# Experts' stage: queries' products and picks stepped inside the experts' loop, the row scale moved into the gates' exponent, norm sums taken from transposed tiles

## The chip, the cores and the metric

The kernel runs on one NeuronCore of a Trainium2 chip. The core has engines with instruction queues of their own: PE (TensorE, matrix products, whose weight loads the profile shows as PEld), DVE (VectorE), ACT (ScalarE), POOL (GpSimd) and SP (SyncE), and 16 DMA engines that move data between HBM and SBUF. Each engine takes its instructions in order and waits on semaphores. The metric is the device time of one execution, in microseconds (us).

## The reference, cut to what matters

Two transformer blocks over 256 tokens of 2048 values, all in float32. The change lies between them: in the expert layer (PEER) of the first block and in the two norms that follow it.

```python
def peer(xn, wq, subkeys, u, v):             # xn = rmsnorm(h, ffn_norm), 256 tokens
    q = (xt @ wq).reshape(T, 8, 2, 128)      # 8 heads, two halves of 128
    s1, s2 = q[:, :, 0] @ subkeys[0].T, q[:, :, 1] @ subkeys[1].T
    v1, i1 = top_k(s1, 16); v2, i2 = top_k(s2, 16)
    cand = (v1[..., :, None] + v2[..., None, :]).reshape(T, 8, 256)
    sc, ci = top_k(cand, 16)                 # 16 experts per head and token
    idx = i1[ci // 16] * 128 + i2[ci % 16]
    gate = softmax(sc)
    h = gelu(einsum('cd,chkd->chk', xc, u[idx]))
    return einsum('chk,chkd->cd', gate * h, v[idx])
h = h + peer(...)
x = rmsnorm(h, final_norm)                   # end of the first block
h2 = rms_norm(x, norm1_w)                    # start of the second
proj = h2 @ w_in                             # z, dt, conv input, q, k, v
```

## The kernel before

The 256 tokens lie as two tiles of 128 partitions (tt = 0 and 1). The weights stream from HBM through `Stream` (L36): chunks of 128x1024 floats (512 KB, `raw`, ring of 4, loaded by SP), each split into a rounded part `hi` on ACT (L64) and a rest `lo` on DVE (L70).

The stage that the change rebuilds is `peer`. It has three kinds of work:

- **Queries** (`queries`): 16 tiles `qT[0..15]` of 128x256, each from two chunks of `wq`. A chunk is 8 pairs of products on PE, L241 (512 columns) and L243 (256 columns). A finished tile is added up by ACT L253 and DVE L257, and multiplied on DVE by the row scale `rb` (L258).
- **Picks** (`picks`, `topk`): for each token tile and head, 16 in all, two small products (L968), then on DVE the best 16 of 128 twice, the best 16 of the 256 sums, and the indices `ix`; ACT takes the exponent of the scores (L1007).
- **Experts** (`experts`): 256 steps (tt, head, k), numbered e0 to e255 here. In each step POOL starts an indirect DMA (L866) that fetches, for each of the 128 tokens, one row of 4096 floats (u and v side by side, 2.1 MB a step) into one of NBUF = 5 buffers `uv`. DVE multiplies the u half with the gained tokens `hg` and sums (L926), ACT takes the gelu (L928), DVE makes the diagonal matrix `dg` (L907), PE adds `dg` times the v half into four PSUM banks (L909, four products, eight matmuls in the trace). The buffer is then free for the fetch four steps ahead. Head hh of tile tt needs the pick of that head before its first fetch.

`mix(queries(), experts(), MIXQ)` writes these out in code order: one step of `experts` for each chunk of the queries until the queries end. `experts` has three such steps for each expert, and more where a pick is missing. The code order isn't the engines' order: the framework puts each engine's instructions in an order of its own when it builds the program, and starts an instruction earlier than the code has it where its inputs and buffers are there. PSUM and SBUF buffers of a tag are handed out in code order.

After e127 `residual(0)` adds the four banks to `h` (L915) and frees them for tile 1; `turn(0, j)` then transposes `h` in 128x128 pieces (L879) and splits them for the second block (ACT L228, DVE L229), and `stats(0, j)` forms the sums of h squared and of (h times `fn`) squared for the two norms, with `fn` loaded from HBM in eight pieces (L893, L895, L212). The same follows for tile 1 after e255, beside the first products of the second block (`self.first`, L274 to L276).

At the start of `peer`, POOL forms `hg` = h times `fg` for both tiles (L825, eight multiplications of 128x512), and `spread` makes `rb` on PE and DVE (L164, L166).

## Time and profile before

| what | value |
|---|---|
| time, median of 3 runs | 2891.52 us (2889.49 to 2894.91) |
| time of the profiled execution | 2895.72 us |
| its span, first to last instruction | 2893.9 us |
| PE, DVE, ACT, POOL busy | 88%, 67%, 32%, 12% of the span |
| mean granted TensorE clock | 0.981 of full speed |
| DMA, mean over the span | 282 GB/s |
| indirect fetches (queue q0) | 536.89 MB, 44.1% of 16 DMA engines over the span |

The span lies 1.8 us under the profiled execution's own time, and that execution lies 4.2 us over the median of the three runs. Busy shares are means over stages with different limits, so the stage in question is read from windows of the trace: its first fetch starts 403 us into the span, its last expert's products end at 1755 us.

### The profile page before, as it was taken

The numbers are of one execution on the slowest core, as the hardware profiler recorded it, in microseconds if no ns is written. First come the engines' busy times: TensorE is split into PE (matmuls) and PEld (weight loads), VectorE is DVE, ScalarE is ACT, GpSimd is POOL, SyncE is SP. The second block draws the span as 40 slices with busy tenths as digits, with TensorE's granted clock in tenths as the row PEclk, the third lists the DMA queues.
The fourth block names the chain that finished last, engine by engine and source line by source line (L and its number), as shares of the span: only waits on it lengthen the run. The fifth ranks groups of instructions, "written<-read, shape, count | busy, mean of one in ns | idle before, by whom it ended". The sixth has DMA issues, their size and how long they took to land.

```text
span 2893.9 us, 29409 instructions
## 1 busy us (share of the span) xinstructions
PE 2554.5 (88%) x10286; PEld 1712.4 (59%) x10286; DVE 1947.3 (67%) x3558; ACT 927.0 (32%) x1665; POOL 349.8 (12%) x314
## 2 busy tenths in 40 slices
PE   9999999768777776877777778999999999999999
PEld 8877776323222222322222227888888888888887
DVE  6778677997555555555555555885668888887444
ACT  6556543221000002000000004555454444444333
POOL 0211031222121112211212110000000000000000
PEclk9999999989999998999999999999999999999999
DMA  8332478989999999999999995545455555555664
GB/s 318 117 102 89 148 277 347 384 320 380 427 428 429 428 428 374 428 428 428 429 428 427 428 428 181 195 132 181 156 182 183 188 187 184 188 184 188 197 195 154
DMA packets 119380, 817.34 MB, mean 282 GB/s; under 512 B 14656, under 2 KB 17600, under 8 KB 85696
## 3 DMA queue, kind: packets, MB, share of 16 engines
q0 software_dynamic: 36864, 536.89, 44.1%
q1 hardware_dynamic: 76032, 271.58, 28.5%
q10 hardware_dynamic: 6336, 6.99, 0.8%
q8 instruction: 81, 1.33, 0.2%
q14 instruction: 67, 0.55, 0.1%
HBM read 813.32 MB, written 2.10 MB: 282 GB/s over the span
## 4 chain that ended last, share of the span: by engine, by line
PE 46%; DMA 30%; issue 9%; DVE 8%; POOL 1%; ACT 1%; POOLq 0%; ACTq 0%; DVEq 0%
DMA uv<-in_uv_dram,ix 28%; PE acc L241 14%; PE acc L243 7%; PE acc L274 7%; PE acc L276 7%; PE acc L275 7%; DVE uv L926 2%; PE acc L909 2%; POOL uv L866 1%; DMA raw<-in_wq_dram 1%; DVE lo L70 1%; DMA fnc<-in_fn_dram 1%; DVE dg L907 0%; DVE tmp L959 0%; ACT hi L64 0%
## 5 line engine op out<-in xcount | busy, mean ns | idle before, releaser
L909 PE MATMUL acc<-uv,dg 128*128 128x512 f32 x2048 | 967.8, 618 | 298.0 <-DVE dg L907 298.0
L909 PEld LDWEIGHTS acc<-uv,dg 128*128 128x128 f32 x2048 | 379.4, 194 | 874.0 <-DVE dg L907 483.6
L926 DVE CUSTOM_DVE_ANT_0 uv<-uv,hg 128x2048 f32<-128x2048 f32 x256 | 586.4, 2291 | 372.9 <-DMA uv<-in_uv_dram,ix 372.8
L70 DVE TENSOR_TENSOR lo<-raw,hi 128x1024 fp32r<-128x1024 f32 (+3 forms) x494 | 597.2, 1210 | 315.5 <-ACT hi L64 314.1
L64 ACT ACTIVATE hi<-raw 128x1024 fp32r<-128x1024 f32 (+3 forms) x506 | 527.8, 1044 | 697.8 <-PE acc L276 270.1
L241 PE MATMUL acc<-xs,hi 128*128 128x512 f32 x1936 | 696.4, 402 | 0.0
L243 PE MATMUL acc<-xs,lo 128*128 128x256 f32 x1936 | 548.6, 283 | 0.0
L928 ACT ACTIVATE g<-d,rs 128x1 f32<-128x1 f32 x256 | 75.3, 294 | 1099.6 <-DVE d L926 1099.5
L241 PEld LDWEIGHTS acc<-xs,hi 128*128 128x128 f32 x1936 | 368.0, 190 | 90.5 <-issue 0.9
L866 POOL DMA_INDIRECT uv<-in_uv_dram,ix x256 | 271.3, 1060 | 1081.0 <-PE acc L909 509.1
L243 PEld LDWEIGHTS acc<-xs,lo 128*128 128x128 f32 x1936 | 367.7, 190 | 1.6 <-issue 0.8
L907 DVE TENSOR_SCALAR dg<-ident,g,gt 128x128 f32<-128x128 f32 x256 | 106.4, 416 | 97.3 <-ACT g L928 91.0
L274 PE MATMUL acc<-hi,xs 128*128 128x512 f32 (+3 forms) x384 | 147.1, 389 | 2.0 <-ACT hi L64 2.0
L275 PE MATMUL acc<-lo,xs 128*128 128x512 f32 (+3 forms) x384 | 144.3, 377 | 4.4 <-DVE lo L70 3.3
L276 PE MATMUL acc<-hi,xs 128*128 128x512 f32 (+3 forms) x384 | 143.0, 377 | 0.0
L276 PE MATMUL acc<-hi,act 128*128 128x512 f32 x352 | 138.7, 394 | 0.0
L274 PE MATMUL acc<-hi,act 128*128 128x512 f32 x352 | 138.7, 394 | 0.0
L275 PE MATMUL acc<-lo,act 128*128 128x512 f32 x352 | 138.7, 394 | 0.0
L241 PE MATMUL m<-xs,hi 128*128 128x512 f32 x256 | 96.5, 416 | 2.4 <-ACT hi L64 2.4
L1339 DVE SCALAR_TENSOR_TENSOR fu<-fup,fw,fu 128x256 f32<-128x256 f32 x176 | 84.8, 482 | 3.1
L275 PEld LDWEIGHTS acc<-lo,xs 128*128 128x128 f32 x384 | 74.0, 193 | 16.0 <-DVE lo L70 5.9
L274 PEld LDWEIGHTS acc<-hi,xs 128*128 128x128 f32 x384 | 73.7, 193 | 13.4 <-ACT hi L64 2.8
(319 smaller groups left out, 2332.0 us busy)
## 6 DMA issues: line engine op xcount, KB each, us to landing
raw<-in_w_up_dram SPq DMA_DIRECT2D x176, 512.0 KB, 3.3
raw<-in_w_dn_dram SPq DMA_DIRECT2D x88, 512.0 KB, 3.4
raw<-in_w_in_dram SPq DMA_DIRECT2D x66, 512.0 KB, 3.5
raw<-in_w_out_dram SPq DMA_DIRECT2D x64, 512.0 KB, 3.4
raw<-in_w_b_dram SPq DMA_DIRECT2D x48, 512.0 KB, 3.3
raw<-in_wq_dram SPq DMA_DIRECT2D x32, 512.0 KB, 4.5
raw<-in_w_z_dram SPq DMA_DIRECT2D x16, 352.0 KB, 3.5
btab<-in_btab_dram SPq DMA_DIRECT2D x4, 1024.0 KB, 7.9
```

The lines of the kernel that those rows point to most:

```text
L64: self.nc.scalar.activation(h[:, :n], r[:, :n], AF.Copy)
L70: e.tensor_tensor(lo[:, :n], r[:, :n], h[:, :n].bitcast(F32), op=ALU.subtract)
L241: nc.tensor.matmul(acc, h[:, s], x.rearrange("p a t -> p (a t)"), start=(kk == 0), stop=False, skip_group_check=True)
L243: nc.tensor.matmul(acc[:, T:], lo[:, s], x[:, 0], start=False, stop=(kk == nk - 1), skip_group_check=True)
L274: nc.tensor.matmul(a, x[:, 0, t], h[:, s], start=(kk == 0), stop=False, skip_group_check=True)
L275: nc.tensor.matmul(a, x[:, 0, t], lo[:, s], start=False, stop=False, skip_group_check=True)
L276: nc.tensor.matmul(a, x[:, 1, t], h[:, s], start=False, stop=(kk == nk - 1), skip_group_check=True)
L866: nc.gpsimd.indirect_dma_start(out=t, out_offset=None, in_=I["uv"], in_offset=bass.IndirectOffsetOnAxis(ap=idx[tt][hh][:, k:k + 1], axis=0))
L907: nc.vector.tensor_scalar(dg, self.ident, g, gate[tt][hh][:, k:k + 1], op0=ALU.mult, op1=ALU.mult)
L909: nc.tensor.matmul(out[tt][c], dg, t[:, D + c * 512:D + c * 512 + 512], start=(hh, k) == (0, 0), stop=(hh, k) == (7, 15), skip_group_check ...
L926: nc.vector.tensor_tensor_reduce(t[:, :D], t[:, :D], hg[:, tt], 1.0, 0.0, op0=ALU.mult, op1=ALU.add, accum_out=d)
L1339: nc.vector.scalar_tensor_tensor(u[a], up[:, j:j + T], w[:, j:j + 1], u[a], op0=ALU.mult, op1=ALU.add)
```

## The change

- **Order of the stage.** `mix` and `experts` are gone. `peer` writes the first two query tiles, then the pick for head 0 and four fetches, three more chunks of queries, and then the loop over the 256 experts. In it an even step writes one chunk of queries, an odd step one sixth of a pick and one step of the work after a tile. A fetch that lacks its pick writes pick steps, and query chunks where those wait.
- **Row scale.** The query tiles are no longer multiplied by `rb`: L258 (16 multiplications of 128x256 on DVE) and the first `spread` are gone. The order of the scores within a row stays, and the gates' exponent takes the row scale as its factor (`scale=r`, and `sm` = -r times the best score).
- **hg.** POOL forms `hg` for tile 0 only; for tile 1 it is `late_gains`, on DVE, written after e72.
- **Norm sums.** `stats` is gone. `turn` squares the transposed pieces on ACT with the gain as factor (16 pieces of 128x128 a token tile), and PE sums them over partitions with products of one column (`sums`); the sixteen loads of `fn` and the products and squares on them are gone. The sum of h squared stays.
- **Change of tile.** `residual(0)` is written in step 129, before the products of e128, instead of at the end of step 128.

```diff
--- before.py
+++ after.py
@@ -28,7 +28,6 @@
...
 MIX1 = 4.2
-MIXQ = 1.0
 MIX3 = 2.0
...
@@ -817,12 +816,19 @@
...
         hg = tk.tile([128, 2, D], F32, name="hg")
+        fgs = {}
+        def gained(tt, j, e):
+            e.tensor_tensor(hg[:, tt, 512 * j:512 * j + 512], h[:, tt, 512 * j:512 * j + 512], fgs.pop((tt, j)),
+                            op=ALU.mult)
+        def gains(tt, j):
+            fgs[tt, j] = fg = pw.tile([128, 512], F32, tag="fg", name="fg")
+            nc.scalar.dma_start(out=fg, in_=I["fg"][:, 512 * j:512 * j + 512])
         for j in range(4):
-            s = slice(512 * j, 512 * j + 512)
-            fg = pw.tile([128, 512], F32, tag="fg", name="fg")
-            nc.scalar.dma_start(out=fg, in_=I["fg"][:, s])
-            for tt in range(2):
-                nc.gpsimd.tensor_tensor(hg[:, tt, s], h[:, tt, s], fg, op=ALU.mult)
+            gains(0, j)
+            gained(0, j, nc.gpsimd)
         skT = tk.tile([128, 2, 128], F32, name="skT")
...
@@ -831,11 +837,7 @@
...
         def ev(i):
-            def f(a):
-                if i == 0:
-                    nm.spread()
-                self.add_halves(qT[i], a, pw, nm.rb)
-            return f
+            return lambda a: self.add_halves(qT[i], a, pw)
...
@@ -849,26 +851,33 @@
...
                     yield from self.until(f"pq{hh}")
-                    yield from self.topk(qT, skT, iota, tt, hh, idx[tt][hh], gate[tt][hh], tk)
+                    yield from self.topk(qT, skT, iota, rs, tt, hh, idx[tt][hh], gate[tt][hh], tk)
                     self.marks.add(f"pk{tt}{hh}")
...
         rows = {}
-        side = self.beside(picks())
+        main = queries()
+        side = picks()
...
             while f"pk{tt}{hh}" not in self.marks:
-                yield next(side)
+                if next(side) is WAIT:
+                    step(main)
             rows[i] = t = uvp.tile([128, 2 * D], F32, tag="uv", name="uv")
...
         n2 = self.nm = Norm(self, None, self.gains[:, 4], self.npool)
-        self.ss2 = self.npool.tile([128, 2, 8], F32, name="ss2")
+        self.ss2 = self.npool.tile([128, 2], F32, name="ss2")
+        fnT = tk.tile([128, 16], F32, name="fnT")
+        nc.vector.tensor_copy(fnT, self.gains[:, 4])
         nc.vector.tensor_tensor(self.gains[:, 4], self.gains[:, 4], self.gains[:, 2], op=ALU.mult)
+        one = tk.tile([128, 1], F32, name="one")
+        nc.vector.memset(one, 1.0)
+        sums = {}
...
@@ -884,16 +893,19 @@
...
-        def stats(tt, j):
+            sq = pw.tile([128, 512], F32, tag="fg", name="sq")
+            for k in range(4):
+                nc.scalar.activation(sq[:, k * 128:k * 128 + 128], p[:, k * 128:k * 128 + 128], AF.Square,
+                                     scale=fnT[:, 4 * j + k:4 * j + k + 1])
+            if j == 0:
+                sums[tt] = self.ps()
+            for k in range(4):
+                nc.tensor.matmul(sums[tt][:, :1], sq[:, k * 128:k * 128 + 128], one, start=(j, k) == (0, 0),
+                                 stop=(j, k) == (3, 3), skip_group_check=True)
+            yield
             self.sumsq(h[:, tt, 512 * j:512 * j + 512], n2.ssp[:, tt, j:j + 1])
-            for q in (2 * j, 2 * j + 1):
-                fn = pw.tile([128, T], F32, tag="fg", name="fnc")
-                cs = slice(T * q, T * q + T)
-                nc.scalar.dma_start(out=fn, in_=I["fn"][:, cs])
-                sq = pw.tile([128, T], F32, tag="a0", name="sq")
-                nc.vector.tensor_tensor(sq, h[:, tt, cs], fn, op=ALU.mult)
-                self.sumsq(sq, self.ss2[:, tt, q:q + 1])
+            if j == 3:
+                nc.vector.tensor_copy(self.ss2[:, tt:tt + 1], sums[tt][:, :1])
             yield
...
@@ -914,42 +926,54 @@
...
-        def experts():
-            after = iter(())
-            for i in range(NBUF - 1):
-                yield from fetch(i)
-            last = None
-            for i, (tt, hh, k) in enumerate(steps):
-                t = rows.pop(i)
-                d = pw.tile([128, 1], F32, tag="d", bufs=4, name="d")
-                g = pw.tile([128, 1], F32, tag="g", bufs=4, name="g")
-                nc.vector.tensor_tensor_reduce(t[:, :D], t[:, :D], hg[:, tt], 1.0, 0.0, op0=ALU.mult, op1=ALU.add,
-                                               accum_out=d)
-                nc.scalar.activation(g, d, AF.Gelu_apprx_tanh, scale=rs[:, tt:tt + 1])
-                if last:
-                    add(*last)
-                last = (i, t, g)
-                yield from fetch(i + NBUF - 1)
-                if i == 128:
-                    residual(0)
-                    n2.xs = [self.new_x(), self.new_x()]
-                    after = chain(*[turn(0, j) for j in range(4)], *[stats(0, j) for j in range(4)])
+        def late_gains():
+            for j in range(4):
+                gains(1, j)
+                yield
+                yield
+                gained(1, j, nc.vector)
+                yield
+        while "pq0" not in self.marks:
+            step(main)
+        for i in range(NBUF - 1):
+            fetch(i)
+        step(main, 3)
+        after = iter(())
+        last = None
+        for i, (tt, hh, k) in enumerate(steps):
+            t = rows.pop(i)
+            d = pw.tile([128, 1], F32, tag="d", bufs=4, name="d")
+            g = pw.tile([128, 1], F32, tag="g", bufs=4, name="g")
+            nc.vector.tensor_tensor_reduce(t[:, :D], t[:, :D], hg[:, tt], 1.0, 0.0, op0=ALU.mult, op1=ALU.add,
+                                           accum_out=d)
+            nc.scalar.activation(g, d, AF.Gelu_apprx_tanh, scale=rs[:, tt:tt + 1])
+            if i == 129:
+                residual(0)
+                n2.xs = [self.new_x(), self.new_x()]
+                after = chain(*[turn(0, j) for j in range(4)])
+            if last:
+                add(*last)
+            last = (i, t, g)
+            fetch(i + NBUF - 1)
+            if i == 72:
+                after = late_gains()
+            if i % 2:
                 step(side)
                 step(after)
-                for _ in range(3):
-                    yield
-            add(*last)
-            drain(after)
-        mix(queries(), experts(), MIXQ)
+            else:
+                step(main)
+        add(*last)
...
         residual(1)
+        sums_g = []
         for j in range(4):
-            drain(turn(1, j))
+            g = turn(1, j)
+            step(g, 2)
+            sums_g.append(g)
             step(self.first, 1 + (j < 3))
-        for j in range(4):
-            drain(stats(1, j))
+        drain(chain(*sums_g))
         ex.close()
...
@@ -960,7 +984,7 @@
...
-    def topk(self, qT, skT, iota, tt, hh, idx, gt, tk):
+    def topk(self, qT, skT, iota, rs, tt, hh, idx, gt, tk):
...
@@ -1003,8 +1027,9 @@
...
         sm = tk.tile([128, 2], F32, tag="sm", name="sm")
-        nc.vector.tensor_scalar(sm[:, 0:1], sc[:, 0:1], -1.0, None, op0=ALU.mult)
-        nc.scalar.activation(gt, sc, AF.Exp, bias=sm[:, 0:1], accum_out=sm[:, 1:2])
+        r = rs[:, tt:tt + 1]
+        nc.vector.tensor_scalar(sm[:, 0:1], sc[:, 0:1], r, -1.0, op0=ALU.mult, op1=ALU.mult)
+        nc.scalar.activation(gt, sc, AF.Exp, bias=sm[:, 0:1], scale=r, accum_out=sm[:, 1:2])
         nc.vector.reciprocal(sm[:, 1:2], sm[:, 1:2])
...
@@ -1020,8 +1045,7 @@
...
         self.rstd(r1, r1, 2, 1.0 / D)
-        nc.vector.tensor_reduce(r2, self.ss2, AX.X, ALU.add)
-        nc.vector.tensor_tensor(r2, r2, r1, op=ALU.mult)
+        nc.vector.tensor_tensor(r2, self.ss2, r1, op=ALU.mult)
         nc.vector.tensor_tensor(r2, r2, r1, op=ALU.mult)
...
```

What stands on the engines now differs from the code order. First DVE from the first query tile to the first pick (`lo` is a chunk's rest, `qT` a query tile, before the change):

```order
L70 TENSOR_TENSOR lo<-raw,hi 128x1024
L257 TENSOR_TENSOR a_3686<-m,a_3686 128x256
L70 TENSOR_TENSOR lo<-raw,hi 128x1024
L258 TENSOR_TENSOR qT_3607<-a_3686,rb 128x256
L70 TENSOR_TENSOR lo<-raw,hi 128x1024 x2
L257 TENSOR_TENSOR a_3735<-m,a_3735 128x256
L258 TENSOR_TENSOR qT_3608<-a_3735,rb 128x256
L957 MAX v<-m 128x8
```

The same place after the change, from the first tile's last chunk to the first MAX:

```order
L69 TENSOR_TENSOR lo<-raw,hi 128x1024
L254 TENSOR_TENSOR qT_3603<-m,a_3682 128x256
L69 TENSOR_TENSOR lo<-raw,hi 128x1024 x2
L822 TENSOR_TENSOR hg<-h,fg 128x512
L69 TENSOR_TENSOR lo<-raw,hi 128x1024
L254 TENSOR_TENSOR qT_3604<-m,a_3730 128x256
L822 TENSOR_TENSOR hg<-h,fg 128x512
L981 MAX v<-m 128x8
```

One addition a tile stands where an addition and a multiplication stood. `late_gains`, written after e72, stands here: two of its four `hg` multiplications come before the first pick's MAX, the other two some rows on, inside that pick.

ACT where query chunks and experts run side by side (`hi` is a chunk's split, `g` an expert's gelu, before the change):

```order
L253 ACTIVATE a_4142<-m 128x256
L64 ACTIVATE hi<-raw 128x1024 x3
L253 ACTIVATE a_4191<-m 128x256
L928 ACTIVATE g<-d,rs 128x1
L64 ACTIVATE hi<-raw 128x1024
L928 ACTIVATE g<-d,rs 128x1
L64 ACTIVATE hi<-raw 128x1024
L253 ACTIVATE a_4261<-m 128x256
L64 ACTIVATE hi<-raw 128x1024
L928 ACTIVATE g<-d,rs 128x1
L64 ACTIVATE hi<-raw 128x1024
```

The same engine after the change, in the middle of the query chunks:

```order
L63 ACTIVATE hi<-raw 128x1024
L252 ACTIVATE a_4526<-m 128x256
L950 ACTIVATE g<-d,rs 128x1
L63 ACTIVATE hi<-raw 128x1024
L950 ACTIVATE g<-d,rs 128x1
L63 ACTIVATE hi<-raw 128x1024
L252 ACTIVATE a_4641<-m 128x256
L950 ACTIVATE g<-d,rs 128x1
L63 ACTIVATE hi<-raw 128x1024
L950 ACTIVATE g<-d,rs 128x1
```

Before, up to three chunks stand in a row ahead of a gelu; after, one chunk stands ahead of each gelu. On PE the first expert's products come after 251 of the 512 query products before and after 245 of them now; the other 261 stand among 6 experts before, the other 267 among 17 now.

DVE's indices `ix` of the sixteen picks stand, before, behind the dot products of e-1, 2, 9, 14, 16, 18, 19, 21, 23, 25, 27, 29, 30, 32, 34, 35 (-1: ahead of e0), and now behind e-1, 1, 4, 10, 16, 20, 22, 24, 26, 27, 29, 31, 131, 133, 135, 137. PE shows it at the change of token tile (L968/L992 are the picks' products, L909/L921 the experts', L879/L888 the transposes, L903 the new sums, before the change):

```order
L909 MATMUL acc<-uv,dg 128x512 x8
L968 MATMUL m<-skT,qT_3619 128x128
L968 MATMUL m<-skT,qT_3620 128x128
L909 MATMUL acc<-uv,dg 128x512 x8
L968 MATMUL m<-skT,qT_3621 128x128
L968 MATMUL m<-skT,qT_3622 128x128
L909 MATMUL acc<-uv,dg 128x512 x404
L879 MATMUL m<-ident,h 128x128 x16
L909 MATMUL acc<-uv,dg 128x512 x512
```

After the change, PE between the products of e0 to e127 and those of e129:

```order
L921 MATMUL acc<-uv,dg 128x512 x424
L888 MATMUL m<-ident,h 128x128 x4
L992 MATMUL m<-skT,qT_3611 128x128
L992 MATMUL m<-skT,qT_3612 128x128
L921 MATMUL acc<-uv,dg 128x512 x4
L903 MATMUL m<-one,sq 128x1
L888 MATMUL m<-ident,h 128x128 x2
L903 MATMUL m<-one,sq 128x1
L888 MATMUL m<-ident,h 128x128 x2
L903 MATMUL m<-one,sq 128x1
L992 MATMUL m<-skT,qT_3613 128x128
```

Four picks that stood ahead of tile 1's start now stand behind the first transposes, whose PSUM buffers of the same tag the code hands out earlier; the new sums stand ahead of the products of e129.

## Rows read from the trace of the kernel before

**Rows 1.** The page's costliest groups: v products, dot products and dg.

```profile
L909 PE MATMUL acc<-uv,dg 128*128 128x512 f32 x2048 | 967.8, 618 | 298.0 <-DVE dg L907 298.0
L926 DVE CUSTOM_DVE_ANT_0 uv<-uv,hg 128x2048 f32<-128x2048 f32 x256 | 586.4, 2291 | 372.9 <-DMA uv<-in_uv_dram,ix 372.8
L907 DVE TENSOR_SCALAR dg<-ident,g,gt 128x128 f32<-128x128 f32 x256 | 106.4, 416 | 97.3 <-ACT g L928 91.0
```

**Rows 2.** Windows, L926 alone: length, DVE busy (two records each), PEclk, DMA share, GB/s.

```profile
413.50:549.40 135.90, 41.26 (x36) 0.97 0.94 383
549.40:641.40 92.00, 32.01 (x28) 0.87 0.81 314
641.40:680.10 38.70, 18.30 (x16) 0.82 0.86 333
680.10:1108.30 428.20, 200.12 (x174) 1.00 1.01 428
1108.30:1167.20 58.90, 22.93 (x20) 0.86 0.88 362
1167.20:1748.50 581.30, 271.42 (x236) 1.00 1.00 425
```

**Rows 3.** Windows: length, PE, PEld, DVE, ACT, POOL busy, PEclk, DMA, GB/s.

```profile
413.50:455.00 41.50, 36.61 (x157) 25.95 (x155) 27.70 (x47) 12.69 (x20) 4.26 (x3) 0.96 1.01 427
455.00:500.00 45.00, 44.38 (x191) 30.57 (x192) 39.73 (x83) 16.66 (x27) 7.00 (x5) 1.00 0.80 300
520.00:660.00 140.00, 96.56 (x201) 40.91 (x202) 139.71 (x545) 41.12 (x69) 32.85 (x21) 0.87 0.86 339
1755.20:1800.00 44.80, 40.01 (x242) 37.67 (x241) 29.91 (x63) 29.29 (x62) 1.42 (x2) 0.98 0.57 168
```

**Rows 4.** DVE's groups, 520 to 660 us: count, busy us, mean ns, idle before.

```profile
L926 DVE CUSTOM_DVE_ANT_0 uv<-uv,hg 128x2048 f32<-128x2048 f32 x21 | 47.8, 2278 | 0.0
L957 DVE MAX8 sc<-cand 128x8 f32<-128x256 f32 x12 | 5.1, 426 | 0.1
```

**Rows 5.** PE's timeline, query and expert products: start and length in us.

```profile
457.24 0.40 PE L241 MATMUL m<-xs,hi 128*128 128x512 f32 x1
...
457.59 0.40 PE L241 MATMUL m<-xs,hi 128*128 128x512 f32 x1
...
458.30 3.60 PE L909 MATMUL acc<-uv,dg 128*128 128x512 f32 x8
```

**Rows 6.** DMA, 400 to 500 us: packets, MB, share; median us to landing.

```profile
q0 software_dynamic: 1639, 23.97, 58.8%
q1 hardware_dynamic: 3456, 11.44, 30.3%
...
raw<-in_wq_dram SPq DMA_DIRECT2D x16, 512.0 KB, 12.9
```

**Rows 7.** DVE's timeline, the dot products of e36 and e41.

```profile
667.64 2.28 DVE L926 CUSTOM_DVE_ANT_0 uv<-uv,hg 128x2048 f32<-128x2048 f32 x1
...
685.72 2.29 DVE L926 CUSTOM_DVE_ANT_0 uv<-uv,hg 128x2048 f32<-128x2048 f32 x1 [2.39 <-DMA uv<-in_uv_dram,ix]
```

**Rows 8.** Timelines of POOL and DVE around the first query tiles.

```profile
372.85 7.16 POOL L825 TENSOR_TENSOR hg<-h,fg 128x512 f32<-128x512 f32 x4 [0.71 <-DMA fg<-in_fg_dram]
...
378.78 2.31 DVE L70 TENSOR_TENSOR lo<-raw,hi 128x1024 fp32r<-128x1024 f32 x1
381.59 1.23 DVE L70 TENSOR_TENSOR lo<-raw,hi 128x1024 fp32r<-128x1024 f32 x1 [0.50 <-ACT hi L64]
```

**Rows 9.** Groups, 1108 to 1170 us, the change of token tile.

```profile
L895 DVE TENSOR_TENSOR sq<-h,fnc 128x256 f32<-128x256 f32 x8 | 3.4, 422 | 14.9 <-DMA fnc<-in_fn_dram 14.9
...
L915 DVE TENSOR_TENSOR h<-acc,h 128x512 f32<-128x512 f32 x4 | 2.7, 688 | 1.2 <-PE acc L909 1.2
...
L229 DVE SCALAR_TENSOR_TENSOR xs<-m,gains,xs 128x128 fp32r<-128x128 f32 x16 | 4.9, 346 | 0.5 <-ACT xs L228 0.4
...
L879 PE MATMUL m<-ident,h 128*128 128x128 f32 x16 | 2.1, 276 | 1.8 <-DVE h L915 1.8
```


## The prediction

> **What bounds the kernel now.** I start with the page's costliest groups: DVE's dot products are 586 us of work, and nearly all the idle time ahead of them, 372.8 us, ends with a fetch's landing [rows 1]. So the stage looks fetch-bound. The windows of the dot products alone say where that holds, since each window holds a known number of experts (two records each) [rows 2]. e0 to e17 take 135.9 us, 7.55 each; e18 to e31 92.0 us, 6.57 each; e32 to e39 38.7 us, 4.84 each. Then e40 to e126 take 428.2 us for 87 experts, 4.92 each, with DMA full at 428 GB/s. e127 to e136 take 58.9 us, 5.89 each, and e137 to e254 581.3 us for 118, 4.93 each.
>
> The floor is 4.92 us an expert, and no order of the work goes below it. Above it lie 135.9 - 18 x 4.92 = 47.3 us in the first stretch, 92.0 - 68.9 = 23.1 in the second, 58.9 - 49.2 = 9.7 at the change of token tile. Of the first, weights that share the DMA engines need 11.44 MB / 428 GB/s = 26.7 us in any order [rows 6]. About 54 us can be had.
>
> The windows of all engines name the bound in each [rows 3]. From 413.5 to 455 us the DMA engines are full (427 GB/s). From 455 to 500 us PE is busy 44.4 of 45 us and DMA moves 300 GB/s: six experts' products stand between blocks of query products, buffers come free late, fetches start late. From 520 to 660 us DVE is busy 139.7 of 140 us with picks, DMA at 339 GB/s.
>
> **The change, part by part.** *Start.* POOL's multiplications for `hg` ran until 380.0 us, and beside them DVE took 2.31 us for a chunk's rest that takes 1.23 alone [rows 8]. Half of them go to DVE: four there, 0.69 us each by the nearest row, an addition of the same shape [rows 9], so 2.8 us. Gained are some 3 us of slowed DVE work, and the row scale's multiplications of the tiles made before the first fetch. Between -3 and +2 us; I take -1.
>
> *e0 to e17.* A pair of query products takes 0.35 us (457.24 to 457.59), an expert's eight matmuls 3.60 [rows 5]. After the first expert's products come 267 query products among 17 experts: 133.5 x 0.35 + 18 x 3.60 = 111.5 us of PE. DMA: 18 x 4.92 + 26.7 = 115.3 us. DVE: an expert costs it 2.29 + 0.42 = 2.7 us [rows 1]. A pick costs 6.9: in 140 us stand 21 dot products and 12 picks (one MAX of `cand` each), (139.7 - 21 x 2.7) / 12 [rows 3, 4]. Four picks, 18 experts and 16 rests of chunks at 1.23 make 48.6 + 27.6 + 19.7 = 96 us. So DMA bounds at 115, with PE close under it. The bounds are 112 (nothing waits) and 136 (as before); the stretch from 413.5 to 455 us ran fetches and weights together at full rate, so I stay near the lower one: 120 us, 15.9 less.
>
> Here a figure of the Trainium skill speaks against the change. The DMA engines moved 428 GB/s over 428 us [rows 2]. The page "SBUF — State Buffer", section "A bandwidth-pool intuition that's wrong (but worth ruling out)", puts the way from HBM to one core at about 358 GB/s, and from DMA to SBUF at 436. By the first, an estimate, 49 MB of fetches and weights would take 137 us, and this stretch would gain nothing; the trace agrees with the second.
>
> *e18 to e31.* Seven picks stand here now, by the order's list, as densely as before. DVE: 7 x 6.9 + 14 x 2.7 = 86.1 us, 5.9 less than 92.0. The bounds are the floor, 68.9, and 92.0.
>
> *e32 to e39.* When the dense picks ended before, four fetched buffers were waiting, and e36 to e41 took 18.05 us for five experts [rows 7]. The same catching up now begins at e32: 18.05 + 3 x 4.92 = 32.8 us, 5.9 less than 38.7. After that the floor holds, as before.
>
> *e127 to e136.* Before, DVE waited 14.9 us here for the loads of `fn`, in order ahead of the experts' dot products [rows 9]; these loads go. In comes DVE work: four picks (27.6 us), beside the 16 splits (0.346 each, 5.5), the four additions of the residual (2.8), the wait for the last products (1.2) [rows 9] and ten experts (27): 64.1 us. The new column sums on PE stand ahead of e129's products and wait for ACT's squares; no row shows such a wait, and it lies between nothing and the 14.9 us that the in-order wait for `fn` cost. I add 3, nearer to nothing, since the squares need no transfer: 67 us, 8.1 more than now. Then buffers are full, and five experts at 18.05 instead of 24.6 us give 6.5 back. Sum +1.6. That the additions of the residual are written one step later costs nothing by itself: they stand behind e127's products as before.
>
> *After e255.* PE is busy 40.0 of the 44.8 us from 1755.2 on, so what is added there counts [rows 3]. Sixteen products of one column come in. By the transposes, 2.1 us for 16 [rows 9], they cost at least 2.1 us; at most 9, with two records each of a transpose's mean 0.276. The loads of `fn` and the products with them leave, which can give back part of the 4.8 us that PE idles. Between -5 and +9; I take +3. The same sixteen for tile 0 cost nothing outside the stretch above: PE has a quarter of each expert free, and if it had not, they would cost the same 2 to 9 us.
>
> The gates' exponent keeps its instructions, one operand more. The four added loads of `fg` (1 MB, 2.4 us at the full rate) lie ahead of the first fetch.
>
> Sum: -1 - 15.9 - 5.9 - 5.9 + 1.6 + 3 = -24.1 us. Against the profiled execution that is 2895.7 - 24.1 = 2871.6; it ran 4.2 us over the median of the three runs, so the median becomes 2891.5 - 24.1 = 2867.4, say 2867.
>
> **The rivals.** *DMA alone bounds.* Picks and query products hide wholly: e0 to e39 take 40 x 4.92 + 26.7 = 223.5 instead of 266.6 us, the change of tile 49.2 instead of 58.9, the tail nothing: 43 + 9.7 less, 2839 us. For it: the full DMA from 413.5 to 455 us. Against: the order still puts seven picks into 14 experts, and DVE at 6.15 us an expert lies over the floor.
>
> *The pacing doesn't do what it says.* ACT has one chunk's split ahead of each gelu now. Where the chunk lands late, gelu, `dg`, the products, the buffer and POOL's next fetch wait behind it. Chunks landed 12.9 us after issue at the median [rows 6]; the ring of four is loaded some three chunks ahead, about 20 us at one chunk an expert, so mostly they should be there. If each is 1.3 us late beyond what the fetches wait anyway, 17 chunks make 22 us: the first stretch keeps its 136 us or a little more, and 2885 to 2892 us come out, which is no change. By the rule of "DMA: Bandwidth & Descriptors", section "Queues, rings and completion order", each DMA engine serves queues in turn, a packet each; with packets of 14.6 and 3.3 KB (23.97 MB / 1639, 11.44 MB / 3456), an estimate gives a chunk each 6.6 us beside a full fetch queue, 112 us for 17, against the 111.5 of PE. The trace fits it from 413.5 to 455 us, but no run shows chunks at just this demand.
>
> *The change of tile becomes the new stall.* PE can't start e129's products before the column sums, those not before ACT's squares, those not before the transposes, and DVE has four picks in between. If each of the four groups costs a whole chain of some 10 us, as long as two experts, 40 us come on: 2907. It decides from 97 us for the ten experts on, 9.7 each. Against: the two engines have other work in these gaps, and the five buffers hide the first 6.5 us.
>
> **How the numbers follow.** Forecast (2855 to 2877): 0.58. DMA alone: 0.12. Pacing lost: 0.15. Stall at the change of tile: 0.05. The rest, 0.10, lies between these. The likeliest time is 2867. The range leaves out the far end of DMA alone, most of the slower half of lost pacing, and the stall: 2848 to 2886. Under 0.2% (5.8 us, about what a measurement of this kernel can tell from no change) nothing counts: faster 0.85 (forecast, DMA alone, the rest, a third of lost pacing), same 0.10, slower 0.05.
>
> **What would show it.** In the windows of the dot products: e0 to e17 near 120 us, e18 to e31 near 86, e32 to e39 near 33, e127 to e136 near 67 with no wait for `fn`, everything else at 4.92 an expert. PE and DMA both near full in the first stretch, ACT without long waits for `raw`. The prediction is wrong if the first stretch stays over 130 us, if the ten experts at the change of tile take over 85, or if PE waits for the sums after e255.

## The result, and the profile after

The changed kernel takes 2851.65 us (median of 4 runs, 2844.37 to 2852.53) beside 2890.51 us for the kernel before (4 runs, 2889.12 to 2894.91): 38.9 us less by the medians, and over the runs a ratio of 0.9857 with an interval of 0.9838 to 0.9877. The forecast was 2867 with a range of 2848 to 2886 and 24.1 us less. The time lies within that range, but under the 2855 to 2877 that had the chance of 0.58. The profiled execution after took 2850.96 us with a span of 2849.2, 44.7 us under the span of before.

The page's costliest groups after (line, engine, operation, count, busy us, mean ns, idle before and what ended it) answer to [rows 1]:

```profile
L921 PE MATMUL acc<-uv,dg 128*128 128x512 f32 x2048 | 968.3, 618 | 282.1 <-DVE dg L919 281.8
L948 DVE CUSTOM_DVE_ANT_0 uv<-uv,hg 128x2048 f32<-128x2048 f32 x256 | 586.4, 2291 | 368.0 <-DMA uv<-in_uv_dram,ix 368.0
L919 DVE TENSOR_SCALAR dg<-ident,g,gt 128x128 f32<-128x128 f32 x256 | 104.7, 409 | 94.1 <-ACT g L950 92.3
```

They hardly moved: most of their 256 repetitions lie in stretches that were at the floor already. The windows show the change. First those of the dot products alone (length, DVE busy, two records each, granted clock, DMA share, GB/s), cut at the starts of e0, e18, e32, e40, e127, e137 and e255 as in [rows 2]:

```profile
408.79:526.21 117.42, 41.26 (x36) 0.97 1.01 427
526.21:614.88 88.67, 32.01 (x28) 0.87 0.85 338
614.88:648.85 33.97, 18.43 (x17) 1.00 0.99 411
648.85:1076.28 427.43, 200.12 (x174) 1.00 1.01 428
1076.28:1142.16 65.88, 22.88 (x21) 0.90 0.93 370
1142.16:1715.75 573.59, 271.38 (x236) 0.99 1.00 424
```

Then windows of all engines (length; PE, PEld, DVE, ACT, POOL busy; clock, DMA share, GB/s), as in [rows 3], the last one as long after e255's start as the last one there:

```profile
408.80:455.00 46.20, 42.38 (x149) 25.47 (x149) 38.80 (x90) 12.74 (x21) 7.75 (x6) 0.93 1.01 428
455.00:500.00 45.00, 44.78 (x177) 28.62 (x176) 37.43 (x89) 13.41 (x22) 10.83 (x7) 1.00 1.01 427
526.20:614.90 88.70, 62.73 (x135) 26.86 (x133) 88.29 (x331) 25.53 (x42) 22.90 (x14) 0.87 0.85 338
1722.40:1767.20 44.80, 44.30 (x290) 43.35 (x289) 28.01 (x57) 29.48 (x63) 1.99 (x2) 1.00 0.54 164
```

Read together, each stretch names its bound. From 455 to 500 us DMA was at 300 GB/s under a full PE; now it runs at 427 beside a PE that is just as full. From 526 to 615 us DVE has 0.4 us to spare in 88.7 and DMA waits for it. Stretch by stretch, against the sum of the prediction:

| term | before, us | after, us | change | forecast |
|---|---|---|---|---|
| start, up to e0 | 413.52 | 408.79 | -4.7 | -1 |
| e0 to e17 | 135.97 | 117.42 | -18.6 | -15.9 |
| e18 to e31 | 91.96 | 88.67 | -3.3 | -5.9 |
| e32 to e39 | 38.72 | 33.97 | -4.8 | -5.9 |
| e40 to e126 | 428.17 | 427.43 | -0.7 | 0 |
| e127 to e254 | 640.20 | 639.47 | -0.7 | +1.6 |
| from e255's start on | 1145.36 | 1133.45 | -11.9 | +3 |

The changes add up to 44.7 us, not 38.9, because the profiled execution of before lies 5.2 us over its median and that of after 0.7 under. The experts' stage came as forecast, within 3 us a stretch. The part after e255, most of which the change does not touch, is 12 us shorter. Most of these 12 us lie in the feed-forward part, whose instructions are the same. Its additions (88 `fup`, L258 before and L257 after: duration min/median/max, first and last start) took 2645.8 - 2154.3 = 491.5 us before and 2601.4 - 2119.1 = 482.3 after. Two views of the kernel before, of tile `fup` and of L241 from 2160 to 2600 us:

```profile
L258 DVE TENSOR_TENSOR fup<-a,rb x88: 425/426/429, 2154.3 to 2645.8; 128x256 f32<-128x256 f32 x88
...
L241 PE MATMUL acc<-xs,hi x1247: 397/397/398, 2159.6 to 2599.9; 128*128 128x512 f32 x179
```

and the same two on the kernel after:

```profile
L257 DVE TENSOR_TENSOR fup<-a,rb x88: 425/426/428, 2119.1 to 2601.4; 128x256 f32<-128x256 f32 x88
...
L240 PE MATMUL acc<-xs,hi x1266: 391/392/392, 2159.7 to 2598.2; 128*128 128x512 f32 x181
```

That is 9.2 of the 11.9 us. PE is busy without a gap in both (25.00 us of each 25) at a granted clock of 1.00; every product of `xs` with `hi` is 5 to 6 ns shorter.

### The profile page after: what moved, and what is told of

Read it like the earlier page. It is cut to its first block, busy times and chain, and to the rows that moved or that the text cites. A ratio compares the mean times of both kernels' runs of the same rounds, so it can differ in the third digit from the quotient of the medians.

```text
span 2849.2 us, 29467 instructions
## 1 busy us (share of the span) xinstructions
PE 2541.2 (89%) x10346; PEld 1710.4 (60%) x10346; DVE 1934.9 (68%) x3532; ACT 926.9 (33%) x1662; POOL 350.4 (12%) x310
## 4 chain that ended last, share of the span: by engine, by line
PE 50%; DMA 29%; DVE 7%; issue 6%; POOL 1%; ACT 1%; POOLq 0%; ACTq 0%; DVEq 0%
DMA uv<-in_uv_dram,ix 28%; PE acc L240 13%; PE acc L242 7%; PE acc L273 7%; PE acc L274 7%; PE acc L275 7%; PE acc L921 4%; DVE uv L948 2%; PE m L240 1%; POOL uv L870 1%; PE m L242 1%; DVE lo L69 0%; DVE dg L919 0%; PE m L562 0%; PE m L569 0%
## 5 line engine op out<-in xcount | busy, mean ns | idle before, releaser
L921 PE MATMUL acc<-uv,dg 128*128 128x512 f32 x2048 | 968.3, 618 | 282.1 <-DVE dg L919 281.8
L921 PEld LDWEIGHTS acc<-uv,dg 128*128 128x128 f32 x2048 | 379.8, 194 | 852.9 <-DVE dg L919 462.3
L240 PE MATMUL acc<-xs,hi 128*128 128x512 f32 x1936 | 682.1, 396 | 0.0
L870 POOL DMA_INDIRECT uv<-in_uv_dram,ix x256 | 276.5, 1080 | 1047.8 <-PE acc L921 474.1
## 6 DMA issues: line engine op xcount, KB each, us to landing
raw<-in_w_z_dram SPq DMA_DIRECT2D x16, 352.0 KB, 10.2
```

What stands on the lines that cost most here:

```text
L240: nc.tensor.matmul(acc, h[:, s], x.rearrange("p a t -> p (a t)"), start=(kk == 0), stop=False, skip_group_check=True)
L870: nc.gpsimd.indirect_dma_start(out=t, out_offset=None, in_=I["uv"], in_offset=bass.IndirectOffsetOnAxis(ap=idx[tt][hh][:, k:k + 1], axis=0))
L921: nc.tensor.matmul(out[tt][c], dg, t[:, D + c * 512:D + c * 512 + 512], start=(hh, k) == (0, 0), stop=(hh, k) == (7, 15), skip_group_check ...
```

## The experiments

Times are medians. The kernel before took 2891.46 us beside e1 to e4, 2893.36 beside e5 to e8 and 2892.51 beside e9 to e12 (15 to 17 runs each); each ratio is to the kernel before of the same group. Windows are cut as above.

**e1: the norm sums alone.** The kernel before, with `turn` and `sums` of the change in place of `stats`, and the smaller `ss2`:

```diff
-        self.ss2 = self.npool.tile([128, 2, 8], F32, name="ss2")
+        self.ss2 = self.npool.tile([128, 2], F32, name="ss2")
...
-                    after = chain(*[turn(0, j) for j in range(4)], *[stats(0, j) for j in range(4)])
+                    after = chain(*[turn(0, j) for j in range(4)])
```

> The kernel before with one part of the change: the norm sums from the transposed tiles, without the loads of fn beside them. Theory: the stretch e127 to e136 loses its wait for fn (58.95 us before) and has no picks in it, so it falls to about 50 us; e127 to e255 falls by 5 us to some 635; the part after e255 loses 2 to 5 us, the idle time of PE ahead of the convolution's products. The feed-forward part stays as before (492 us from its first to its last fup addition). About 2882 in all. Rival (the sums part also carries the 9.3 us that the feed-forward part was shorter in the profile of after): 2872 to 2874, and a pair of its products takes 0.348 instead of 0.353 us.

Measured: 2872.18 us, ratio 0.9932 (0.9915 to 0.995), 19.3 us less. The change of tile behaved as the theory has it, a little better: the window of its ten experts

```profile
1108.35:1157.30 48.95, 22.94 (x21) 0.97 1.01 426
```

runs at the DMA's full rate, and e127 to e254 took 630.3 us, 9.9 less than before. But the feed-forward part took 482.2 us: the rival holds. Whatever quickens those products comes with the sums. The 2 to 5 us that the theory had after e255 are not there: without the feed-forward part that stretch took 651.7 us, beside 653.9 before (651.1 in e4).

**e2: the row scale alone.** The kernel before with `add_halves(qT[i], a, pw)` and the scale in the gates' exponent:

```diff
-        nc.scalar.activation(gt, sc, AF.Exp, bias=sm[:, 0:1], accum_out=sm[:, 1:2])
+        nc.scalar.activation(gt, sc, AF.Exp, bias=sm[:, 0:1], scale=r, accum_out=sm[:, 1:2])
```

> The kernel before with one part of the change: the row scale in the gates' exponent instead of the query halves. Theory: 16 multiplications and the spread leave DVE and PE where PE bounds (44.4 of 45 us busy), so only the start moves: -1 to -3 us, 2888 to 2890. Rival (the scale's operations stood between query products and picks, and so held much of e0 to e17): e0 to e17 falls from 136 to 130 or less, 2884 or less.

Measured: 2889.34 us, ratio 0.9994 (0.998 to 1.0007). e0 to e17 took 134.4 us, the start 413.74. The scale alone is worth nothing that can be measured, not at the start either, and the rival falls.

**e3: everything but the norm sums.** The changed kernel with the old `stats`, its loads of `fn` and the old `ss2`:

```diff
-            after = chain(*[turn(0, j) for j in range(4)])
+            after = chain(*[turn(0, j) for j in range(4)], *[stats(0, j) for j in range(4)])
```

> The changed kernel with the old norm sums put back: fn is loaded and multiplied again at the change of tile and after e255. Theory: e0 to e126 as in after; e127 to e255 5 to 8 us longer (the wait for fn beside the four picks); after e255 2 to 5 us longer, all of it ahead of the convolution's products; the feed-forward part as in after. 2859 to 2865. Rival (the sums part carries what the feed-forward part gained): 9 us more, 2868 to 2874, with pairs of 0.353 us there.

Measured: 2872.48 us, ratio 0.9936 (0.9918 to 0.9953), 20.8 over after. Each window from e0 to e126 is that of after within 2 us, e127 to e136 took 75.1 us and e127 to e254 649.8, 10.3 longer than after, where the theory had 5 to 8. The group of DVE from 1072 to 1147 us shows why:

```profile
L899 DVE TENSOR_TENSOR sq<-h,fnc 128x256 f32<-128x256 f32 x8 | 3.3, 419 | 10.1 <-DMA fnc<-in_fn_dram 10.1
```

The feed-forward part took 491.5 us again, so the rival holds here too. e1 took off 19.3 us and e3, all the rest of the change, 19.0: the two add up to 38.3, beside 38.9 for the whole.

**e4: the kernel before once more.** No edit.

> The kernel before, unchanged, profiled once more. In the profile of before a pair of products of xs with hi and lo took 0.353 us in every stage, from 28 us on, in that of after 0.348. Theory: that pace belongs to an execution, not to the program, and this one may show 0.348 too, with a feed-forward part nearer 483 than 492 us. Rival: it belongs to the program, and 0.353 and 492 come again.

Measured: 2892.28 us. Feed-forward part 491.5 us, L241 at 397 ns: the theory that this kernel's pace belongs to an execution falls; the rival, that it belongs to the program, holds. The start was 412.44 and e0 to e17 138.7 us here, so two profiles of one program differ by 1 to 3 us in a stretch; from e255's start on it took 1142.6, not 1145.4.

**e5: the query products ahead of the loop.**

```diff
-        step(main, 3)
+        drain(main)
```

> The changed kernel with all the query products written ahead of the experts' loop, not paced beside it. Theory (pacing is what gave e0 to e17 its 18.6 us): PE runs 47 us of query products in a block, behind the first four fetches; DMA then stands between; e0 to e17 goes back to 130 to 136 us, 2862 to 2870 in all. Rival (the gain of that stretch is from the scale and from DVE, not from the pacing): it stays at 117 to 120 us, 2850 to 2855.

Measured: 2882.72 us, ratio 0.9965 (0.9952 to 0.9977), 31.1 over after, more than expected. Windows of all engines:

```profile
415.00:455.00 40.00, 34.18 (x165) 28.17 (x165) 24.31 (x26) 14.53 (x22) 0.00 (x0) 0.87 0.81 312
455.00:500.00 45.00, 43.93 (x166) 26.51 (x164) 29.94 (x85) 9.89 (x16) 10.32 (x8) 1.00 0.78 299
```

While PE makes query tiles no buffer comes free. After its first five fetches POOL waits 67.6 us for the products of an expert and issues none from 405 to 472 us:

```profile
472.19 0.94 POOL L870 DMA_INDIRECT uv<-in_uv_dram,ix  x1 [67.58 <-PE acc L921]
```

e0 to e17 takes 155.6 us; a part comes back (e18 to e31 takes 74.9, with four picks in it instead of seven), and e0 to e39 is 269.9 - 240.1 = 29.8 us longer than in after. So the place of the query products is what this stretch hangs on.

**e6: the picks tied to the dot products.** The order puts twelve picks before e32 (the expectation has e30) and four at the change of tile, though the code steps them evenly. Here each part of a pick reads a column of the newest dot product:

```diff
+            self.lastd = d
...
+            if self.lastd is not None:
+                nc.vector.tensor_copy(v[:, a, 0:1], self.lastd)
             self.top16(v[:, a], ix[:, a], p[:, a * 128:a * 128 + 128], tmp[:, :128])
...
+        if self.lastd is not None:
+            nc.vector.tensor_copy(sc[:, 0:1], self.lastd)
         self.top16(sc, ci, cand.rearrange("p a b -> p (a b)"), tmp)
```

> The changed kernel with each part of a pick tied to the newest dot product by a copy of one column on DVE, so that a pick stands after each twelfth dot product (5, 15, 27 and so on to 171) and not twelve of them before e30 and four at the change of tile. Theory (dense picks make DVE the bound of e18 to e31 and of the change of tile): e18 to e39 takes 22 x 4.92 = 108 us instead of 122.7, e127 to e136 some 50 to 53 instead of 65.9, e127 to e255 near 635. About 2832. Rival (a pick of 6.9 us in a block between two dot products costs a fetch each time): 14 picks at 2 us each, 28 us, eat it, 2850 to 2860.

Measured: 2829.33 us, ratio 0.9784 (0.9766 to 0.9802), 22.3 under after. The windows of its dot products (L949):

```profile
407.12:521.48 114.36, 41.27 (x37) 0.99 1.01 427
521.48:588.85 67.37, 32.17 (x29) 0.95 1.01 428
588.85:630.24 41.39, 18.41 (x16) 1.00 1.01 429
630.24:1058.89 428.65, 200.00 (x175) 0.94 1.00 425
1058.89:1113.42 54.53, 22.93 (x20) 0.98 0.99 404
```

e18 to e31 falls from 88.7 to 67.4 us, the floor of DMA; the catching up after it is gone (41.4 for 34.0), and a pick between two dot products costs e40 to e126 next to nothing: 428.7 for 427.4. With 108.8 us for e18 to e39, where 108 were expected, the theory holds.

**e7: hg at the start, on POOL, as before.**

```diff
+            nc.gpsimd.tensor_tensor(hg[:, 1, 512 * j:512 * j + 512], h[:, 1, 512 * j:512 * j + 512], fgs[0, j],
+                                    op=ALU.mult)
...
-            if i == 72:
-                after = late_gains()
```

> The changed kernel with both tiles of hg multiplied on POOL at the start, as before the change. Theory: the start, e0, comes 2 to 4 us later (DVE's rests of chunks beside POOL's work run at 2.31 us again), the rest as in after, with four DVE multiplications less near e72 that cost nothing: 2854 to 2856. Rival (the start came earlier from the scale or from the execution's pace): within 1 us of after.

Measured: 2854.38 us, ratio 0.9865 (0.9844 to 0.9886). The total is in the expected range, but not for the reason given: the start came at 404.13 us, 4.7 earlier than in after, and e0 to e39 took 246.6 us instead of 240.1. Neither theory nor rival has that. What makes e0 to e39 longer is not known.

**e8: a step of the picks at each expert.**

```diff
-            if i % 2:
-                step(side)
+            step(side)
+            if i % 2:
```

> The changed kernel with a step of the picks at each expert, not at every other, so that all sixteen picks stand before e34 and none at the change of tile. Theory: the dense stretch grows to e16 to e33 and costs four more picks there, 4 to 7 us, and e127 to e136 falls from 65.9 to some 50 us, of which the following experts gave back most; in all -2 to +5 us, 2850 to 2857. Rival (the transposes and the new column sums, not the picks, hold the change of tile): e127 to e136 stays at 60 us or more and the whole is 4 to 7 us slower.

Measured: 2851.43 us, ratio 0.9858 (0.9837 to 0.9878), no change from after. Windows of the dot products:

```profile
526.37:618.37 92.00, 32.08 (x28) 0.86 0.84 326
618.37:655.07 36.70, 18.34 (x17) 0.94 0.90 355
...
1081.38:1131.33 49.95, 22.96 (x20) 1.00 1.01 429
```

As the theory says: without picks the change of tile is at the floor, with the transposes and column sums in it, and e127 to e254 is 8.3 us shorter (631.2); the four picks, two of them now before e18, make e0 to e39 7.9 us longer (248.0). Dense picks cost about the same wherever they stand; spreading them hides them (e6).

**e9, e10, e11: where xs lies.** `ss2` takes 64 bytes of a partition in the old form and 8 in the new, which are laid out as 32. So `h` and `xs`, which stand behind it, lie 32 bytes lower in the new form: `xs` starts at byte 62656 of a partition in before, e2, e3 and e4, and at 62624 in after, e1, e5 to e8 and e12. Here unused numbers move it without any other edit, on before by 32 bytes (e9), on after by 32 (e10), on before by 64 (e11):

```diff
+        pad = self.npool.tile([128, 8], F32, name="pad")
+        nc.vector.memset(pad, 0.0)
         r1 = self.npool.tile([128, 2], F32, name="r1")
```

> The kernel before with a tile of 8 unused numbers (32 bytes in a partition) put into the pool of the norms, in front of h, xs and all that is placed behind them. In the kernels with the smaller ss2 (64 bytes to 32 in the layout), xs starts at byte 62624 of a partition, in those with the old one at 62656, and the feed-forward part took 482.3 us in the former, 491.5 in the latter. Theory: the place of xs sets the pace of its products, and the arithmetic of the norm sums has no part in it. With xs at 62688, as far from a multiple of 64 as in the changed kernel, a pair of products takes 0.348 us, the feed-forward part 482, and the whole 2878 to 2881. Rival (the loads of fn or the sums themselves leave something behind that slows the products): 0.353, 491.5, and 2890 to 2892.

> The changed kernel with the same 32 unused bytes, which put xs back to 62656. Theory: pairs of 0.353 us, a feed-forward part of 491.5, the part after e255 at 1142 to 1143 us, the start 1 to 3 us later, 2861 to 2866 in all, with the windows of the experts as in after. Rival (the place has no part): 482.3 and 2849 to 2854.

> The kernel before with 64 unused bytes there, so that xs starts at 62720, a multiple of 64 and of 128. Theory (multiples of 64 are the slower place): the feed-forward part takes 491.5 us, as before. Rivals: what counts is 128 (62656 is an odd multiple of 64), or any other place than 62656 is good: 482.

The same two views of e9 (xs at 62688), from 2160 to 2600 us for the products:

```profile
L258 DVE TENSOR_TENSOR fup<-a,rb x88: 425/426/428, 2150.0 to 2632.3; 128x256 f32<-128x256 f32 x88
...
L241 PE MATMUL acc<-xs,hi x1271: 392/392/392, 2159.7 to 2600.0; 128*128 128x512 f32 x182
```

on e10 (62656 again):

```profile
L257 DVE TENSOR_TENSOR fup<-a,rb x88: 425/426/429, 2118.3 to 2609.9; 128x256 f32<-128x256 f32 x88
...
L240 PE MATMUL acc<-xs,hi x1247: 397/397/398, 2159.7 to 2600.0; 128*128 128x512 f32 x179
```

and on e11 (62720):

```profile
L258 DVE TENSOR_TENSOR fup<-a,rb x88: 425/426/428, 2148.8 to 2631.1; 128x256 f32<-128x256 f32 x88
...
L241 PE MATMUL acc<-xs,hi x1270: 391/391/391, 2159.9 to 2599.9; 128*128 128x512 f32 x182
```

The feed-forward part took 482.3, 491.6 and 482.3 us. There the layout sets the pace, and the arithmetic of the sums has no part in it. The rule of 64 falls with e11, which took 2880.01 us in its one run, 12 under before. e10 took 2861.84 us (0.9896, 0.988 to 0.9911), 10.2 over after, in the expected range. In its profile the part from e255's start on took 1140.6 us, 7.1 over after, where some 9 were expected; its start was not later but at 405.58, and its e127 to e254 took 644.3, which is not explained.

The byte of `xs` is no rule by itself, though. `xs` has three buffers, 16384 bytes apart, and 62656 is only the middle one: the feed-forward part reads the two others, which move with it. And the 192 products of `xs` with `hi` early in the second block behave otherwise. Here they are in before, after, e9 and e11, with the first and last start:

```profile
L241 PE MATMUL acc<-xs,hi x192: 389/397/402, 1812.5 to 1880.0; 128*128 128x512 f32 x192
...
L240 PE MATMUL acc<-xs,hi x192: 391/392/395, 1775.2 to 1841.4; 128*128 128x512 f32 x192
...
L241 PE MATMUL acc<-xs,hi x192: 392/392/402, 1804.9 to 1872.4; 128*128 128x512 f32 x192
...
L241 PE MATMUL acc<-xs,hi x192: 388/398/403, 1808.6 to 1876.1; 128*128 128x512 f32 x192
```

They take 67.5 us before and 66.2 after, but 67.5 also in e9 and e11, whose feed-forward part is fast. So only two of the four layouts have one pace throughout: 62656 was slow in both places in each of five profiles, 62624 fast in both in each of seven. With 62688 and 62720 both paces stand in one execution, and what chooses between them is open.

e9 contradicts the theory in its total: the profiled execution took 2883.19 us, near the expected 2878 to 2881, but the other twelve lay between 2894.6 and 2902.3, and the median is 2897.71 (1.0021, 1.0011 to 1.003). A feed-forward part at the slower pace would make 9.2 of these some 14 us; no trace of those twelve exists, so this is not shown.

**e12: no picks around the change of tile.** e6 with

```diff
-                step(side)
+                if not 112 <= i < 140:
+                    step(side)
```

> The kernel with the tied picks, and no step of the picks from the 112th to the 139th expert, so that they stand after dot products 111 and 151 and none in between. Theory (the picks at 123 and 135 are what is left over the floor at the change of tile): e127 to e136 falls from 54.5 to 49 to 50 us, e127 to e255 from 633.4 to 630 to 631, 2825 to 2828 in all. Rival (the transposes, squares and column sums hold the 54.5): no change, 2828 to 2831.

Measured: 2828.2 us, ratio 0.9777 (0.9762 to 0.9792). Windows of the dot products, e127 to e136 and then to e254:

```profile
1060.73:1110.60 49.87, 22.95 (x20) 1.00 1.00 423
1110.60:1692.86 582.26, 271.36 (x237) 0.97 1.00 422
```

The ten experts take 49.9 us as the theory says, but the rest runs at 422 GB/s, so that e127 to e254 took 632.1 us for e6's 633.4, where 630 to 631 were expected. From e6 it can't be told by its time; both beat the kernel before by 2.2%.

## Why the prediction was right, and where it was off

**Start (-1, measured -4.7).** The 4.7 us are not the change's. They stand already at the first addition into `h`, ahead of `peer`, in code that the change leaves as it is (before, then after):

```profile
249.74 0.68 DVE L305 TENSOR_TENSOR h<-acc,h 128x512 f32<-128x512 f32 x1
...
245.03 0.68 DVE L304 TENSOR_TENSOR h<-acc,h 128x512 f32<-128x512 f32 x1
```

From there to e0 both take 163.8 us, so the term that the prediction worked out, -3 to +2, came out at nothing. That addition started between 241.8 and 250.4 us over all the kernels, and what moves it is open. The pace of `xs` isn't it: e3 and e10 have the slow one and reach this point at 242.8 and 242.0. e7 puts a price on `hg`: with both tiles on POOL the stretch to e0 takes 158.8 us, and 160.9 to 163.8 in the kernels that share the changed `hg`. By this one profile the move to DVE cost 2 to 5 us there and gained nothing.

**e0 to e17 (120, measured 117.4).** Right, and by the bounds that were named: DMA at 427 GB/s for the whole stretch, PE busy 113.4 of 117.4 us. The rival of lost pacing is out: ACT's splits (hi, the wait behind the last arrow is the one for chunks) waited 0.4 us for DMA from 408.8 to 526.2 us, though a chunk of `wq` took 15.6 us to land there at the median, longer than before [rows 6].

```profile
L63 ACT ACTIVATE hi<-raw 128x1024 fp32r<-128x1024 f32 (+1 forms) x18 | 18.2, 1011 | 28.7 <-PE m L240 24.8 <-issue 3.4 <-DMA raw<-in_wq_dram 0.4
```

e5 puts a price on the pacing: 29.8 us over e0 to e39 when the products stand ahead. That the order of the stage gave these 18.6 us follows by elimination: the scale alone leaves the stretch at 134.4 us (e2) and the sums alone at 140.8 (e1), while without the new sums (e3) or the moved `hg` (e7) it stays at 117.2 and 118.6. The estimate of 6.6 us for a chunk beside a full queue of fetches holds too. From 408.8 to 455 us the fetches (q0) and the weights (q1) moved nearly the same number of packets, and 3.91 MB of weights in 46.2 us make 6.2 us a chunk:

```profile
q0 software_dynamic: 1080, 15.86, 80.2%
q1 hardware_dynamic: 1083, 3.91, 20.7%
```

The rate also settles the weighing against the 358 GB/s of the Trainium skill, page "SBUF — State Buffer", section "A bandwidth-pool intuition that's wrong (but worth ruling out)": over these 117 us the trace shows 427 GB/s.

**e18 to e31 (86.1, measured 88.7).** Right: DVE was busy 88.3 us. Counted as in the prediction a pick took (88.3 - 37.8) / 7 = 7.2 us here, not 6.9. The rival that DMA alone bounds failed here, and e6 shows what it would have needed: the same experts with the picks spread take 67.4, and e0 to e39 takes 223.1 where that rival has 223.5.

**e32 to e39 (32.8, measured 34.0).** Right, by the buffers that wait full at the end of the dense stretch: e32 to e35 follow within 3.2 us of each other, and e36 is the first whose dot product waits for its fetch.

**The change of tile (67, measured 65.9).** Right. The work counted for DVE was 64.1 us, it was busy 62.7, and e137 to e254 gave back 7.7 us, where 6.5 were counted. Removing the loads of `fn` gave 9.9 us (e1) or 10.3 (e3), the four picks took that back (65.9 beside 49.9 without them, e8). The feared stall of the column sums is not there; PE waited 1.3 us for the squares in the whole change of tile (its products of one column, idle before):

```profile
L903 PE MATMUL m<-one,sq 128*128 128x1 f32 x32 | 4.3, 242 | 1.3 <-ACT sq L898 1.3
```

**After e255 (+3, between -5 and +9; measured -11.9).** This is the step that failed. It counted the products that come in and the waits that leave near the change. These stayed within its bounds: the window of 44.8 us has PE busy 44.3 instead of 40.0 [rows 3], and the sixteen products took 4.0 us there without a wait of PE for the squares.

```profile
L903 PE MATMUL m<-one,sq 128*128 128x1 f32 x32 | 4.0, 229 | 0.0
```

Outside the feed-forward part the sum is 1133.4 - 482.3 = 651.1 us, beside 653.9 and 651.1 in the two profiles of before: next to nothing, where +3 was taken. What the step left out is 9.2 us of unchanged products in the feed-forward part, and 1.3 us of those early in the second block, which run faster because `ss2` is smaller and `h` and `xs` lie 32 bytes lower (e1, e3, e10). The step took it for granted that code which the change doesn't touch keeps its pace.

By e10 the change without this shift is worth 2892.51 - 2861.84 = 30.7 us, against the 24.1 forecast. The shift was not foreseen, and it took the time away from the likeliest 2867, not towards it: without its 9.2 us 2861 would have come out.

## What to carry to other kernels

A stage is read stretch by stretch, each with its own bound: before the change this one was bound by PE, by DVE, by DMA and, at the change of tile, by the loads of `fn`, while the page's costliest groups pointed to the fetches alone. Stepping side work evenly in the code doesn't place it evenly on an engine; look at the order of the instructions, and where it bunches, tie the work to something that comes late, which was worth 22 us here. When a stretch that a change doesn't touch changes its time, look first where in the trace the difference begins, and compare where the tiles lie before looking for a mechanism in the change.

## What the runs showed of the hardware

The layout of SBUF can set the pace of matrix products. In the feed-forward part a product of `xs` and `hi` took 397 ns in the layout with `xs` at byte 62656 and 391 to 392 ns in those with 62624, 62688 and 62720, at a granted clock of 1.00 in both before and after; that is 9.2 us over the part. `hi` and `lo` lie at the same bytes in all of them, so that of what these products read only `xs` moved. In the layouts with 62688 and 62720 the products early in the second block took as long as before (67.5 us), so that no rule for the place follows. Where a queue of fetches and a queue of weights were both full, they moved 1080 and 1083 packets in 46.2 us, nearly a packet of one for a packet of the other, though the packets were of 14.7 and 3.6 KB at the mean.
